# A Mamba-2 (SSD) scan stage: the sample sequences' states by products on quarters of the rows, and the D x term by VectorE

## The chip, the cores and the metric

One core of a Trainium2 chip runs the whole kernel in one launch. The metric is the device time of that core in microseconds (us), shown as the median of several runs.

## The reference, cut to what matters

One step of an encoder with two layers: a Mamba-2 mixer and a PEER channel mixer, then sliding-window attention and a second PEER mixer. Only the scan of the first layer is touched. `x` is the convolved input, `z` the gate; 32 heads of 64 columns stand in 8 groups of 4.

```python
def ssd_scan(x, dt, A, B, C, s0, block):
    acum = jnp.cumsum(dt * A.reshape(G, R), axis=2)
    lmat = jnp.exp(jnp.where(causal, seg, -jnp.inf))
    xdt = x * dt[..., None]
    cb = jnp.einsum('bcign,bcjgn->bcijg', C, B)
    y_diag = jnp.einsum('bcijgr,bcjgrp->bcigrp', cb[..., None] * lmat, xdt)
    decay_end = jnp.exp(acum[:, :, -1:] - acum)
    states = jnp.einsum('bcjgn,bcjgrp->bcgrpn', B, xdt * decay_end[..., None])
    # s = dec * s + st over the blocks; s_prev is the state before a block
    y_off = jnp.einsum('bcign,bcgrpn->bcigrp', C, s_prev) * jnp.exp(acum)[..., None]
    y = (y_diag + y_off)
# mamba_mixer:
    y = y + xs.astype(f32) * d_skip.astype(f32)[:, None]     # the D x term
    y = y.reshape(bsz, L, SSM_INNER) * jax.nn.silu(z.astype(f32))
    y = rmsnorm(y, norm_g)
    return y @ w_out, s_new, conv_new
```

There are 384 tokens: two blocks of 128 of one prompt, and one block that holds 8 sample sequences of 16 tokens. Each sample sequence has a state of its own, so the last block has 8 states per group, each 128 x 256.

## The kernel before, in words

The functions run one after another: `mamba()`, the first PEER mixer, `attention()`, the second PEER mixer. The order of the instructions on each engine isn't that of the code: a scheduler lays out the program by times that it estimates, and only instructions wrapped in `pin` keep the order of the code among each other. PSUM is one pool of 8 banks (`bank`).

Matmuls with weights are done in three fp32r products of high and low halves (L130 to L132); the halves are made by ScalarE (L105) and VectorE (L106). In `mamba()` a loop runs over the 8 groups. For each group:

- `b_tile`, `c_tile` and two `x_tile`s: each is a `conv_tile`, 24 matmuls (L130 to L132), then a convolution of four taps (VectorE L371) and a silu on ScalarE. POOL copies a few columns for the convolution's state (L362, L365, L366), and `c_tile` has it spread C for the sample sequences (L409).
- `gate`: 72 matmuls with w_z (L425 to L427), silu on ScalarE into `zs`.
- `fetch`: loads the row of the decay sums into `ab` (L391) and the sample states `s0` (L394, 1 MB), and has POOL write two diagonal matrices `dg` of D (L397).
- `decay`: 12 VectorE instructions on `ab` (L438), Exp on ScalarE (L441), C·B (L444), their product (L446), and B transposed (L449). `Bt` has 2 slices for the prompt's blocks and 8 for the sample block, each with the rows of one sequence and zeros elsewhere (8 ScalarE copies, L453).
- `tokens`: x transposed (L461), times dt and times the decay to the end, `xdt` and `xde` (VectorE L463).
- `states` (L471 to L475), and `outputs`: `pY` sums, for each half of each block, one product with the diagonal (L483, which is the D x term) and two products of `ab` and `xdt` (L487). `pO` takes the states' share: one product for prompt block 1 (L490), and for the sample block 8 products on 32 columns each (L494). VectorE then forms y in four steps: pO times the decay (L499), block 0 (L501), plus pY (L502), times the gate (L503). ScalarE squares y (L505).
- `turn`: y transposed, two banks of three blocks each (L512), split into `yhi`, `ylo` (ScalarE L108, VectorE L109).
- `carry`: s0 times its decay (VectorE L518), 8 products of full 128 rows with the masked `Bt` (L523), four additions (L525).
- `store`: the states go out by SP's queue (L528, L529, 1 MB).

The outputs, turn and carry of a group stand in the code between the tiles of the next group; those of the last group stand between the terms of the GEMM with w_out (`out_terms`), whose accumulators `accs` hold 6 of the 8 banks until the hidden state h is updated (L600). Then the first PEER mixer squares h (ScalarE L164), normalises it (VectorE L839, tile `qTp`), transposes it (L850) and starts its GEMM with p_w_q (L130 to L132 on `qhi`, `qlo`).

Of the kernel before, what the change touches and what calls it, by code (L numbers as in the profile page):

```python
# [9 lines left out]
F32 = mybir.dt.float32  # L10
# [5 lines left out]
AF = mybir.ActivationFunctionType  # L16
OP = mybir.AluOpType
AX = mybir.AxisListType

P = 128  # L20
D = 1024
KD = D // P
NB = 3
NP = 256
NT = NB * P
NSEQ = 8
# [32 lines left out]
def encoder_step(ctx: ExitStack, tc: tile.TileContext, t_in, t_out):  # L59
# [149 lines left out]
    def mamba(h_src):  # L209
        with ExitStack() as c:  # L210
# [42 lines left out]
            alog = brow(t_in["a_log"], HEADS, one, "alog")  # L253
            ng = T(one, [P, 16], F32, tag="ng")
            sync.dma_start(ng, t_in["m_norm"])
            dsk = T(one, [P, 16], F32, tag="dsk")
            sync.dma_start(dsk, t_in["d_skip"])

            ylo = T(y_pool, [P, 16, NT], F32R, tag="ylo")
            yhi = T(y_pool, [P, 16, NT], F32R, tag="yhi")  # L260
# [7 lines left out]
            decS = T(one, [P, NSEQ, HEADS], F32, tag="decS")  # L268
            rows = T(dram, [HEADS, NB, P], F32, tag="acum_rows")
            seqm = T(one, [P, NSEQ], F32, tag="seqm")  # L270
            msk = T(one, [P, NB, P], F32, tag="msk")
            CMS = []
            for i in range(2):
# [3 lines left out]
            if True:  # L277
                def steps():
# [11 lines left out]
                    same = T(one, [P, P], F32, tag="same")  # L290
                    dve.tensor_scalar(same, fif, seqf, None, op0=OP.is_equal)
                    dve.tensor_scalar(seqm, iob[:, :NSEQ], seqf, None, op0=OP.is_equal)
                    ones = T(one, [P, P], F32, tag="ones")
                    pool.memset(ones, 1.0)
                    tri = T(one, [P, P], F32, tag="tri")
# [84 lines left out]
                class Group:  # L380
# [6 lines left out]
                    def fetch(self):  # L387
                        g = self.g
                        self.ab = T(two, [P, 4, NB, P], F32, tag="ab")
                        src = rows[4 * g:4 * g + 4]  # L390
                        sync.dma_start(self.ab, bass.AP(tensor=src.tensor, offset=src.offset,  # L391
                                                        ap=[[0, P], [1, 4 * NB * P]]))
                        self.s0 = T(two, [P, NSEQ, 256], F32, tag="s0")
                        sync.dma_start(self.s0, t_in["state_ssm"][g])  # L394
                        self.dg = T(two, [P, 2, P], F32, tag="dg", bufs=1)
                        for j in range(2):
                            pool.tensor_scalar(self.dg[:, j], ident, dsk[:, 2 * g + j:2 * g + j + 1], None, op0=OP.mult)  # L397

                    def b_tile(self):
                        self.BT = T(two, [P, NT], F32, tag="BT")  # L400
# [31 lines left out]
                    def decay(self):  # L432

                        g, BT, CT = self.g, self.BT, self.CT
                        ab = self.ab
                        for rr in range(4):
                            for b in range(NB):
                                dve.scalar_tensor_tensor(ab[:, rr, b], ab[:, rr, b],  # L438
                                                         acum[:, b, 4 * g + rr:4 * g + rr + 1], msk[:, b],
                                                         op0=OP.subtract, op1=OP.add)  # L440
                        act.activation(ab, ab, AF.Exp)  # L441
                        cb = bank([P, NB, P])
                        for b in range(NB):
                            pe.matmul(cb[:, b], BT[:, b * P:(b + 1) * P], CT[:, b * P:(b + 1) * P],  # L444
                                      start=True, stop=True)
                        dve.tensor_tensor(ab, ab, cb[:, None].to_broadcast([P, 4, NB, P]), op=OP.mult)  # L446
                        pb = bank([P, NB, P])
                        for b in range(NB):
                            pe.transpose(pb[:, b], BT[:, b * P:(b + 1) * P], ident)  # L449
                        self.Bt = Bt = T(two, [P, 2 + NSEQ, P], F32, tag="Bt", bufs=1)  # L450
                        act.copy(Bt[:, 0:2], pb[:, 0:2])
                        for i in range(NSEQ):
                            act.activation(Bt[:, 2 + i], pb[:, 2], AF.Copy, scale=seqm[:, i:i + 1])  # L453

                    def tokens(self):
                        self.xdt = T(two, [P, NB, 256], F32, tag="xdt", bufs=1)
                        self.xde = T(two, [P, NB, 256], F32, tag="xde", bufs=1)
                        for b in range(NB):
                            px = bank([P, 256])
                            for j in range(2):  # L460
                                pe.transpose(px[:, j * P:(j + 1) * P], self.xs[:, j, b * P:(b + 1) * P], ident)  # L461
                            for o, sc in ((self.xdt, dt), (self.xde, ddt)):
                                dve.tensor_tensor(heads(o[:, b]), heads(px),  # L463
                                                  sc[:, b, self.hs].unsqueeze(2).to_broadcast([P, 4, 64]), op=OP.mult)

                    def states(self):

# [9 lines left out]
                    def outputs(self):  # L477
                        g = self.g
                        pY = [bank([P, 256]), bank([P, 2, 256])]
                        for b in range(NB):  # L480
                            o = pY[0] if b == 0 else pY[1][:, b - 1]
                            for j in range(2):
                                pe.matmul(o[:, j * P:(j + 1) * P], self.xs[:, j, b * P:(b + 1) * P], self.dg[:, j],  # L483
                                          start=True, stop=False)
                                for rr in (2 * j, 2 * j + 1):
                                    cs = slice(64 * rr, 64 * rr + 64)
                                    pe.matmul(o[:, cs], self.ab[:, rr, b], self.xdt[:, b, cs], start=False,  # L487
                                              stop=(rr == 2 * j + 1))
                        pO = bank([P, 2, 256])
                        pe.matmul(pO[:, 0], self.CT[:, P:2 * P], self.st[:, 0], start=True, stop=True)  # L490
                        for w in range(2):
                            for q in range(4):
# [1 line left out]
                                pe.matmul(pO[rows, 1], self.CM[:, w, q].rearrange("p w t -> p (w t)"),  # L494
                                          self.s0[:, 2 * q + w], start=(w == 0), stop=(w == 1),
                                          tile_position=(0, 32 * q))
                        y = self.y = T(two, [P, NB, 256], F32, tag="y", bufs=1)
                        y12 = y[:, 1:].rearrange("p b (r d) -> p b r d", d=64)
                        dve.tensor_tensor(y12, pO.rearrange("p b (r d) -> p b r d", d=64),  # L499
                                          etok[:, :, self.hs].unsqueeze(3).to_broadcast([P, 2, 4, 64]), op=OP.mult)  # L500
                        dve.tensor_tensor(y[:, 0], self.zs[:, 0], pY[0], op=OP.mult)  # L501
                        dve.tensor_tensor(y[:, 1:], y[:, 1:], pY[1], op=OP.add)  # L502
                        dve.tensor_tensor(y[:, 1:], y[:, 1:], self.zs[:, 1:], op=OP.mult)  # L503
                        for b in range(NB):
                            act.activation(self.zs[:, b], y[:, b], AF.Square, accum_out=ssq[:, b, g:g + 1])  # L505

# [8 lines left out]
                    def carry(self):  # L515
# [3 lines left out]
                                          s0.rearrange("p s (r d) -> p s r d", d=64),  # L519
                                          decS[:, :, self.hs].unsqueeze(3).to_broadcast([P, NSEQ, 4, 64]), op=OP.mult)  # L520
                        pss = [bank([P, 2, 256]) for _ in range(4)]
                        for i in range(NSEQ):
                            pe.matmul(pss[i // 2][:, i % 2], self.Bt[:, 2 + i], self.xde[:, 2], start=True, stop=True)  # L523
                        for k in range(4):
                            dve.tensor_tensor(s0[:, 2 * k:2 * k + 2], s0[:, 2 * k:2 * k + 2], pss[k], op=OP.add)  # L525

# [738 lines left out]
def _layout(i):  # L1265
# [20 lines left out]
    a["conv_b"] = f["m_conv_b"][0].reshape(32, P).T  # L1286
    a["dt_bias"] = f["m_dt_bias"][0]
    a["a_log"] = f["m_a_log"][0]
    a["d_skip"] = np.repeat(f["m_d_skip"][0], 64).reshape(16, P).T
    a["m_norm"] = f["m_norm"][0].reshape(16, P).T  # L1290
    a["w_out"] = f["m_w_out"][0]
    a["state_conv"] = f["state_conv"][0].reshape(NSEQ, 3, 32, P).transpose(3, 2, 0, 1)
# [54 lines left out]
```

## Time and profile before

| what | value |
|---|---|
| time, median of 3 runs (lowest to highest) | 2598.19 us (2575.7 to 2599.0) |
| the profiled execution: its time, its span | 2597.6 us, 2595.9 us |
| its mean granted TensorE clock | 0.976 of full speed |
| PE busy | 2449.1 us, 94% |
| DVE busy | 1941.7 us, 75% |
| ACT busy | 1323.8 us, 51% |
| POOL busy | 685.0 us, 26% |

PE is TensorE (a matmul of fp32 operands stands in the trace as two records), DVE VectorE, ACT ScalarE, POOL GpSimd, SP the queue engine that issues most transfers. The span is the time between the first and the last instruction of the profiled execution; its own time, 1.7 us longer, holds what lies around it. The scan of the 8 groups runs from about 30 to 330 us of the span, the GEMM with w_out to about 398 us.

### The profile page before, as it was taken

How to read it: one execution, taken by the hardware profiler on the slowest of the kernel's cores; microseconds unless marked ns; L12 is line 12 of the kernel's file. 1: busy time of each engine (PE TensorE's matmuls, PEld its weight loads, DVE VectorE, ACT ScalarE, POOL GpSimd, SP SyncE). 2: the span in 40 equal slices, each digit the busy share in tenths (PEclk: the TensorE clock that was granted, in tenths of full speed). 3: DMA queues.
4: the chain of work that ended last, by engine and by line, in shares of the span. 5: the costliest groups of instructions: out<-in, count | busy, mean ns of one | idle time of the engine just before them, and what ended most of it. 6: DMA issues, size and time to landing. Idle time of an engine off the chain costs nothing. (4 is left out here: it accounts for less than half of the span.)

```text
span 2595.9 us, 45141 instructions
## 1 busy us (share of the span) xinstructions
PE 2449.1 (94%) x16792; PEld 2070.4 (80%) x16792; DVE 1941.7 (75%) x4301; ACT 1323.8 (51%) x2562; POOL 685.0 (26%) x749
## 2 busy tenths in 40 slices
PE   7999999999899989999998999999899998899998
PEld 7999988988799966666666878998789976666666
DVE  6877737989899988765545655989989988775545
ACT  5655524433466665554444543434456666464444
POOL 2222200033322244333321100023332234433331
PEclk9999999999999999999998969999999999999999
DMA  4544444488888899888985204478888898988886
GB/s 182 203 148 178 144 135 145 151 282 273 271 305 293 292 340 349 330 308 296 322 307 179 92 9 150 137 253 280 269 286 287 296 323 311 364 294 294 321 315 233
DMA packets 179116, 645.62 MB, mean 249 GB/s; under 512 B 24192, under 2 KB 26096, under 8 KB 176240
## 3 DMA queue, kind: packets, MB, share of 16 engines
q1 hardware_dynamic: 99632, 366.90, 40.2%
q0 software_dynamic: 79264, 275.84, 30.5%
q8 instruction: 131, 2.15, 0.3%
q14 instruction: 89, 0.73, 0.1%
HBM read 626.43 MB, written 18.06 MB: 248 GB/s over the span
## 5 line engine op out<-in xcount | busy, mean ns | idle before, releaser
L105 ACT CAST hi<-raw 128x1024 fp32r<-128x1024 f32 (+1 forms) x616 | 641.3, 1042 | 652.8 <-PE bank L131 407.4
L106 DVE TENSOR_TENSOR lo<-raw,hi 128x1024 fp32r<-128x1024 f32 (+1 forms) x616 | 748.8, 1216 | 225.2 <-ACT hi L105 213.6
L1035 POOL DMA_INDIRECT gath<-in_p_u,eidU x256 | 301.9, 1179 | 803.3 <-DVE gath L1072 438.8
L132 PE MATMUL bank<-xhi,lo 128*128 128x256 f32 (+1 forms) x1344 | 407.5, 304 | 9.9 <-DVE lo L106 9.7
L130 PE MATMUL bank<-xhi,hi 128*128 128x256 f32 (+1 forms) x1344 | 402.3, 299 | 4.2 <-ACT hi L105 4.2
L131 PE MATMUL bank<-xlo,hi 128*128 128x256 f32 (+1 forms) x1344 | 396.7, 295 | 0.0
L132 PE MATMUL bank<-qhi,lo 128*128 128x256 f32 (+1 forms) x1152 | 348.9, 305 | 27.1 <-DVE lo L106 26.9
L130 PE MATMUL bank<-qhi,hi 128*128 128x256 f32 (+1 forms) x1152 | 348.1, 302 | 20.4 <-ACT hi L105 13.6
L1072 DVE SCALAR_TENSOR_TENSOR gath<-gath,xg 128x1024 f32<-128x1024 f32 x256 | 311.5, 1217 | 44.0 <-DMA gath<-in_p_u,eidU 43.9
L131 PE MATMUL bank<-qlo,hi 128*128 128x256 f32 (+1 forms) x1152 | 343.9, 299 | 0.0
L143 PE MATMUL bank<-lo,phi 128*128 128x512 f32 x1024 | 332.3, 406 | 10.2 <-DVE lo L106 8.2
L143 PE MATMUL bank<-hi,plo 128*128 128x512 f32 x1024 | 323.9, 398 | 0.0
L143 PE MATMUL bank<-hi,phi 128*128 128x512 f32 x1024 | 292.8, 406 | 19.4 <-ACT hi L105 16.1
L105 ACT CAST phi<-G 128x256 fp32r<-128x256 f32 x256 | 103.4, 405 | 382.0 <-PE bank L143 264.4
L1035 POOL DMA_INDIRECT gv<-in_p_v,eidT x180 | 202.1, 1123 | 319.0 <-PE bank L1089 273.6
L132 PEld LDWEIGHTS bank<-xhi,lo 128*128 128x128 f32 x1344 | 253.8, 189 | 18.0 <-DVE lo L106 14.1
L143 PEld LDWEIGHTS bank<-hi,phi 128*128 128x128 f32 x1024 | 186.9, 190 | 98.7 <-ACT hi L105 45.6
L130 PEld LDWEIGHTS bank<-xhi,hi 128*128 128x128 f32 x1344 | 254.3, 189 | 8.6 <-ACT hi L105 5.6
L131 PEld LDWEIGHTS bank<-xlo,hi 128*128 128x128 f32 x1344 | 254.1, 189 | 0.2
L132 PEld LDWEIGHTS bank<-qhi,lo 128*128 128x128 f32 x1152 | 222.9, 194 | 34.0 <-DVE lo L106 33.7
L143 PEld LDWEIGHTS bank<-lo,phi 128*128 128x128 f32 x1024 | 187.4, 190 | 73.2 <-DVE lo L106 18.3
L130 PEld LDWEIGHTS bank<-qhi,hi 128*128 128x128 f32 x1152 | 223.7, 194 | 24.3 <-ACT hi L105 16.7
(340 smaller groups left out, 3949.0 us busy)
## 6 DMA issues: line engine op xcount, KB each, us to landing
raw<-in_u_t SPq DMA_DIRECT2D x256, 512.0 KB
raw<-in_p_v SPq DMA_DIRECT2D x256, 512.0 KB
raw<-in_w_in SPq DMA_DIRECT2D x32, 512.0 KB
raw<-in_p_w_q SPq DMA_DIRECT2D x32, 512.0 KB
s<-in_state_ssm SPq DMA_DIRECT2D x8, 1024.0 KB
raw<-in_w_z SPq DMA_DIRECT2D x16, 512.0 KB
out_sm_ssm<-s SPq DMA_DIRECT2D x8, 1024.0 KB
raw<-in_w_out SPq DMA_DIRECT2D x16, 512.0 KB
```

Of the source, the lines that this page charges most:

```text
L105: act.copy(hi, raw)
L106: dve.tensor_tensor(lo, raw, hi32, op=OP.subtract)
L130: pe.matmul(ps, whi[:, s], xhi[:, k, c0:c1], start=(k == 0), stop=False)
L131: pe.matmul(ps, whi[:, s], xlo[:, k, c0:c1], start=False, stop=False)
L132: pe.matmul(ps, wlo[:, s], xhi[:, k, c0:c1], start=False, stop=(k == KD - 1))
L143: mm = pe.matmul(ps, x, w[:, hf * n:(hf + 1) * n], start=s_, stop=e_)
L1035: pool.indirect_dma_start(out=tile_, out_offset=None, in_=tab, in_offset=bass.IndirectOffsetOnAxis(ap=idx, axis=0))
L1072: pin(dve.scalar_tensor_tensor(tile_, tile_, 1.0, xg[g], op0=OP.mult, op1=OP.mult, accum_out=au[g][:, j:j + 1]))
```

## The change

The D x term leaves TensorE. `d_skip` is loaded as a row of 32 values, `dg` and its POOL instructions go, and so do the 48 products with it; `tokens` has VectorE write x times D into `y`, from the bank that it also reads for `xdt` and `xde`. `outputs` then adds: pO times the decay goes to a new tile `yo`, POOL adds `yo` to blocks 1 and 2 of `y`, VectorE adds the two pY banks and multiplies all three blocks by the gate in one instruction.

The states of the sample sequences: two sequences stand in each quarter of 32 rows. `Bt` now has two masked slices, one with the even and one with the odd sequences (mask `parm`). A product takes 32 rows of `Bt` and of `xde`, in the quarter q of the array's rows. The 8 products are pinned: all four quarters of the even sequences, each into its own bank, then the four of the odd ones.

```diff
-            dsk = T(one, [P, 16], F32, tag="dsk")
-            sync.dma_start(dsk, t_in["d_skip"])
+            dsk = brow(t_in["d_skip"], HEADS, one, "dsk")
...
+                    dve.tensor_reduce(parm, seqm.rearrange("p (q w) -> p w q", w=2), axis=AX.X, op=OP.add)
...
-                        self.dg = T(two, [P, 2, P], F32, tag="dg", bufs=1)
-                        for j in range(2):
-                            pool.tensor_scalar(self.dg[:, j], ident, dsk[:, 2 * g + j:2 * g + j + 1], None, op0=OP.mult)
...
-                        self.Bt = Bt = T(two, [P, 2 + NSEQ, P], F32, tag="Bt", bufs=1)
+                        self.Bt = Bt = T(two, [P, 4, P], F32, tag="Bt", bufs=1)
                         act.copy(Bt[:, 0:2], pb[:, 0:2])
-                        for i in range(NSEQ):
-                            act.activation(Bt[:, 2 + i], pb[:, 2], AF.Copy, scale=seqm[:, i:i + 1])
+                        for w in range(2):
+                            act.activation(Bt[:, 2 + w], pb[:, 2], AF.Copy, scale=parm[:, w:w + 1])
...
+                            dve.tensor_tensor(heads(self.y[:, b]), heads(px),
+                                              dsk[:, self.hs].unsqueeze(2).to_broadcast([P, 4, 64]), op=OP.mult)
...
-                            for j in range(2):
-                                pe.matmul(o[:, j * P:(j + 1) * P], self.xs[:, j, b * P:(b + 1) * P], self.dg[:, j],
-                                          start=True, stop=False)
-                                for rr in (2 * j, 2 * j + 1):
-                                    cs = slice(64 * rr, 64 * rr + 64)
-                                    pe.matmul(o[:, cs], self.ab[:, rr, b], self.xdt[:, b, cs], start=False,
-                                              stop=(rr == 2 * j + 1))
+                            for rr in range(4):
+                                cs = slice(64 * rr, 64 * rr + 64)
+                                pe.matmul(o[:, cs], self.ab[:, rr, b], self.xdt[:, b, cs], start=True, stop=True)
...
-                        y = self.y = T(two, [P, NB, 256], F32, tag="y", bufs=1)
-                        y12 = y[:, 1:].rearrange("p b (r d) -> p b r d", d=64)
-                        dve.tensor_tensor(y12, pO.rearrange("p b (r d) -> p b r d", d=64),
+                        y = self.y
+                        yo = T(two, [P, 2, 256], F32, tag="yo", bufs=1)
+                        dve.tensor_tensor(yo.rearrange("p b (r d) -> p b r d", d=64),
+                                          pO.rearrange("p b (r d) -> p b r d", d=64),
                                           etok[:, :, self.hs].unsqueeze(3).to_broadcast([P, 2, 4, 64]), op=OP.mult)
-                        dve.tensor_tensor(y[:, 0], self.zs[:, 0], pY[0], op=OP.mult)
+                        pool.tensor_tensor(y[:, 1:], y[:, 1:], yo, op=OP.add)
+                        dve.tensor_tensor(y[:, 0], y[:, 0], pY[0], op=OP.add)
                         dve.tensor_tensor(y[:, 1:], y[:, 1:], pY[1], op=OP.add)
-                        dve.tensor_tensor(y[:, 1:], y[:, 1:], self.zs[:, 1:], op=OP.mult)
+                        dve.tensor_tensor(y, y, self.zs, op=OP.mult)
...
-                        for i in range(NSEQ):
-                            pe.matmul(pss[i // 2][:, i % 2], self.Bt[:, 2 + i], self.xde[:, 2], start=True, stop=True)
+                        for w in range(2):
+                            for q in range(4):
+                                rows = slice(32 * q, 32 * q + 32)
+                                pin(pe.matmul(pss[q][:, w], self.Bt[rows, 2 + w], self.xde[rows, 2],
+                                              start=True, stop=True, tile_position=(32 * q, 0)))
```

Lines after the edits stand a few lines lower: L499, L502 and L503 of before answer to L497, L502 and L503, L438 to L437, L490 to L488, L494 to L492, L523 to L525, L525 to L528, L529 to L532, L600 to L603, L839 to L842, L850 to L853.

The scheduler lays the instructions out anew. On TensorE, in the turn of a group in mid-program (group 5), before: `xhi`, `xlo` rows are the conv tiles' matmuls (24 to a tile, shortened here), `ident` rows the transposes of `y`.

```order
L490 MATMUL bank_2787<-st_2760,CT_2397 128x256
L494 MATMUL bank_2787<-s_373_2347,cm_55_248 32x256 x8
L130 MATMUL bank_2806<-xhi_100,hi_2809 128x384
...
L132 MATMUL bank_2806<-xhi_100,lo_2810 128x384
L512 MATMUL bank_2853<-ident_69,y_2797 128x128
L512 MATMUL bank_2859<-ident_69,y_2797 128x128
...
L523 MATMUL bank_2912<-xde_2691,Bt_2587 128x256 x2
...
L512 MATMUL bank_2853<-ident_69,y_2797 128x128 x2
L512 MATMUL bank_2859<-ident_69,y_2797 128x128 x2
```

The same place now:

```order
L488 MATMUL bank_2725<-st_2704,CT_2346 128x256
L492 MATMUL bank_2725<-s_374_2304,cm_56_249 32x256 x8
L130 MATMUL bank_2745<-xhi_100,hi_2748 128x384
...
L132 MATMUL bank_2745<-xhi_100,lo_2749 128x384
L512 MATMUL bank_2792<-ident_69,y_2635 128x128 x3
L512 MATMUL bank_2798<-ident_69,y_2635 128x128 x3
L130 MATMUL bank_2805<-xhi_100,hi_2808 128x384
...
L525 MATMUL bank_2851<-xde_2634,Bt_2536 128x256
L525 MATMUL bank_2852<-xde_2634,Bt_2536 128x256
```

Before, one transpose per bank (block 0) stands behind the next conv tile's 24 matmuls, and the other four behind a second conv tile and the states' products. Now all six stand behind the first conv tile. Group 0 has all six directly behind the products of pO.

On VectorE at the same place, from pO's first reader on, before:

```order
L499 TENSOR_TENSOR y_2797<-bank_2787,etok_240 128x512
L518 TENSOR_TENSOR s_373_2347<-s_373_2347,decS_242 128x2048
L502 TENSOR_TENSOR y_2797<-y_2797,bank_2768 128x512
L438 SCALAR_TENSOR_TENSOR ab_3161<-ab_3161,acum_238,msk_245 128x128 x12
L503 TENSOR_TENSOR y_2797<-y_2797,zs_2684 128x512
```

and now (L502 waits for POOL's addition, L500, which waits for L497):

```order
L497 TENSOR_TENSOR yo_2735<-bank_2725,etok_240 128x512
L518 TENSOR_TENSOR s_374_2304<-s_374_2304,decS_242 128x2048
L502 TENSOR_TENSOR y_2635<-y_2635,bank_2712 128x512
L437 SCALAR_TENSOR_TENSOR ab_3098<-ab_3098,acum_238,msk_246 128x128 x12
L503 TENSOR_TENSOR y_2635<-y_2635,zs_2627 128x768
```

The order is the same; the last step now covers block 0 too, so that no block of y is ready before it. Groups 1 to 5 read so; in group 6 the 12 L437 don't stand ahead of L503.

On VectorE at the end of the w_out GEMM: before, h is updated (L600) and normalised (L839) without a break:

```order
L600 SCALAR_TENSOR_TENSOR h_90<-bank_3525,rs_3993,h_90 128x512
L600 SCALAR_TENSOR_TENSOR h_90<-bank_3526,rs_3993,h_90 128x512
L839 TENSOR_SCALAR qTp_4025<-h_90,rstd_4030 128x1024
...
L600 SCALAR_TENSOR_TENSOR h_90<-bank_3527,rs_3993,h_90 128x512
L600 SCALAR_TENSOR_TENSOR h_90<-bank_3528,rs_3993,h_90 128x512
L839 TENSOR_SCALAR qTp_4025<-h_90,rstd_4030 128x1024
```

and now:

```order
L603 SCALAR_TENSOR_TENSOR h_90<-bank_3454,rs_3915,h_90 128x512
L166 TENSOR_TENSOR ss_3950<-ss_627_3951 128x1
L528 TENSOR_TENSOR s_494_3100<-s_494_3100,bank_3677 128x512
L167 TENSOR_SCALAR ss_3950<-ss_3950 128x1
L528 TENSOR_TENSOR s_494_3100<-s_494_3100,bank_3678 128x512
L528 TENSOR_TENSOR s_494_3100<-s_494_3100,bank_3679 128x512
L528 TENSOR_TENSOR s_494_3100<-s_494_3100,bank_3680 128x512
L603 SCALAR_TENSOR_TENSOR h_90<-bank_3455,rs_3915,h_90 128x512
L166 TENSOR_TENSOR ss_3950<-ss_627_3951 128x1
L167 TENSOR_SCALAR ss_3950<-ss_3950 128x1
L842 TENSOR_SCALAR qTp_3947<-h_90,rstd_3952 128x1024 x3
```

The last group's states' products now fill four banks at once, and two of the four come free only when h is updated; the last six of the eight products stand behind nearly all of the w_out GEMM, the additions between the updates of h, and all three L842 behind them. The first L842 waits, besides, for the store of these states (L532), because its tile lies where the scan's buffers lay. Before, that store stood some 30 us earlier.

## Rows read from the trace of the kernel before

**Rows 1.** The page: each engine's busy time, share of the span and instructions.
```profile
PE 2449.1 (94%) x16792; PEld 2070.4 (80%) x16792; DVE 1941.7 (75%) x4301; ACT 1323.8 (51%) x2562; POOL 685.0 (26%) x749
```

**Rows 2.** Busy time of the engines in stretches of the scan: from:to, length in us, then busy us of PE, weight loads, DVE, ACT, POOL with instruction counts, PE's granted clock, DMA share, GB/s.
```profile
80.00:130.00 50.00, 49.48 (x354) 47.22 (x353) 42.15 (x74) 34.60 (x75) 8.98 (x26) 1.00 0.59 214
...
230.00:280.00 50.00, 50.00 (x360) 48.48 (x360) 40.37 (x65) 32.48 (x73) 12.89 (x31) 1.00 0.52 188
```

**Rows 3.** The timeline of PE in one group: start us, us, engine, line, operation, tiles, shape, count of records.
```profile
213.72 0.44 PE L483 MATMUL bank<-dg,xs 128*128 128x128 f32 x2
214.00 0.56 PE L487 MATMUL bank<-xdt,ab 128*128 128x64 f32 x4
214.39 0.44 PE L483 MATMUL bank<-dg,xs 128*128 128x128 f32 x2
...
216.31 1.07 PE L494 MATMUL bank<-s,cm 128*32 128x256 f32 x16
217.31 0.45 PE L130 MATMUL bank<-xhi,hi 128*128 128x384 f32 x1
...
221.58 0.38 PE L512 MATMUL bank<-ident,y 128*128 128x128 f32 x2
...
226.04 3.62 PE L523 MATMUL bank<-xde,Bt 128*128 128x256 f32 x16
229.49 0.60 PE L512 MATMUL bank<-ident,y 128*128 128x128 f32 x4
```

**Rows 4.** Groups of instructions of the first 620 us, shapes kept apart: line, engine, operation, tiles, shapes, count | busy us, mean ns of one | idle before.
```profile
L523 PEld LDWEIGHTS bank<-xde,Bt 128*128 128x128 f32 x128 | 24.1, 190 | 3.1
L397 POOL TENSOR_SCALAR dg<-ident,dsk 128x128 f32<-128x128 f32 x16 | 11.4, 720 | 11.7 <-PE bank L483 11.7
L463 DVE TENSOR_TENSOR xde<-bank,ddt 128x256 f32<-128x256 f32 x24 | 9.9, 414 | 0.0
```

**Rows 5.** The timeline of DVE in the same group (columns as in rows 3; in brackets the idle time before, and who ended it).
```profile
217.45 0.69 DVE L499 TENSOR_TENSOR y<-bank,etok 128x512 f32<-128x512 f32 x1 [1.43 <-PE bank L494]
218.06 2.28 DVE L518 TENSOR_TENSOR s<-s,decS 128x2048 f32<-128x2048 f32 x1
220.25 0.68 DVE L502 TENSOR_TENSOR y<-y,bank 128x512 f32<-128x512 f32 x1
220.85 3.23 DVE L438 SCALAR_TENSOR_TENSOR ab<-ab,acum,msk 128x128 f32<-128x128 f32 x12
224.01 0.68 DVE L503 TENSOR_TENSOR y<-y,zs 128x512 f32<-128x512 f32 x1
224.61 1.21 DVE L106 TENSOR_TENSOR lo<-raw,hi 128x1024 fp32r<-128x1024 f32 x1
```

**Rows 6.** The timeline of POOL there.
```profile
216.47 0.60 POOL L397 TENSOR_SCALAR dg<-ident,dsk 128x128 f32<-128x128 f32 x1
...
222.99 2.88 POOL L365 COPY cst<-xp 128x3 f32<-128x3 f32 x1 [5.72 <-ACT xp L363]
...
228.78 0.19 POOL L365 COPY cst<-xp 128x3 f32<-128x3 f32 x1 [2.34 <-ACT xp L363]
...
232.95 0.41 POOL L409 COPY cm<-CT 128x64 f32<-128x64 f32 x2 [1.95 <-ACT CT L374]
```

**Rows 7.** The timeline of PE in group 0's turn.
```profile
73.30 1.07 PE L494 MATMUL bank<-s,cm 128*32 128x256 f32 x16
...
74.58 3.62 PE L523 MATMUL bank<-xde,Bt 128*128 128x256 f32 x16
77.85 0.53 PE L130 MATMUL bank<-xhi,hi 128*128 128x384 f32 x1
```

**Rows 8.** The timeline of DVE there.
```profile
82.38 1.28 DVE L525 TENSOR_TENSOR s<-s,bank 128x512 f32<-128x512 f32 x2
83.58 0.68 DVE L503 TENSOR_TENSOR y<-y,zs 128x512 f32<-128x512 f32 x1
```

**Rows 9.** PE after a gap, at the start of the first PEER mixer.
```profile
406.64 0.69 PE L130 MATMUL bank<-qhi,hi 128*128 128x384 f32 x1 [3.63 <-ACT xf L852]
...
410.33 0.52 PE L132 MATMUL bank<-qhi,lo 128*128 128x384 f32 x1
410.65 0.47 PE L130 MATMUL bank<-qhi,hi 128*128 128x384 f32 x1
```

**Rows 10.** Stretches around two gaps of PE of 3.6 and 3.2 us (columns as in rows 2).
```profile
403.00:411.00 8.00, 4.37 (x15) 4.36 (x15) 6.47 (x10) 6.14 (x15) 0.00 (x0) 0.57 0.49 170
...
2119.00:2123.00 4.00, 0.84 (x8) 0.17 (x10) 2.72 (x4) 0.53 (x1) 0.93 (x1) 1.00 1.03 416
```

**Rows 11.** The timeline of DVE at the end of the w_out GEMM.
```profile
392.32 1.41 DVE L600 SCALAR_TENSOR_TENSOR h<-bank,rs,h 128x512 f32<-128x512 f32 x2 [1.13 <-PE bank L143]
...
401.11 0.75 DVE L839 TENSOR_SCALAR qTp<-h,rstd 128x1024 f32<-128x1024 f32 x1 [0.65 <-POOL rstd L168]
```

**Rows 12.** SP's queue: a store of a group's states, and the next load into the same buffer, which waits for it; twice.
```profile
120.22 0.34 SPq L529 DMA_DIRECT2D out_sm_ssm<-s  x1
124.43 0.33 SPq L394 DMA_DIRECT2D s<-in_state_ssm  x1
...
194.87 0.34 SPq L529 DMA_DIRECT2D out_sm_ssm<-s  x1
200.39 0.33 SPq L394 DMA_DIRECT2D s<-in_state_ssm  x1
```

More of the change, by code (lines that the diff above doesn't have):

```diff
@@ L270, in mamba @@
             seqm = T(one, [P, NSEQ], F32, tag="seqm")
+            parm = T(one, [P, 2], F32, tag="parm")
             msk = T(one, [P, NB, P], F32, tag="msk")
@@ L457, in tokens @@
                         self.xde = T(two, [P, NB, 256], F32, tag="xde", bufs=1)
+                        self.y = T(two, [P, NB, 256], F32, tag="y", bufs=1)
                         for b in range(NB):
@@ L1288, in _layout @@
     a["a_log"] = f["m_a_log"][0]
-    a["d_skip"] = np.repeat(f["m_d_skip"][0], 64).reshape(16, P).T
+    a["d_skip"] = f["m_d_skip"][0]
     a["m_norm"] = f["m_norm"][0].reshape(16, P).T
```

## The prediction

> **What bounds the kernel now.** I read the page first: PE is busy 94% of the span, DVE 75% [rows 1]. That average hides stages, so the stretches of the scan came next. There PE is busy 49.5 to 50.0 of every 50 us at a granted clock of 1.00, with DVE at 40 to 42, ACT at 32 to 35 and POOL at 9 to 13 [rows 2]. In the scan PE sets the time: work taken off PE shortens it, work put on DVE costs nothing until PE has to wait for it. So the question is what PE waits for after the change, and the order of the instructions answers more of it than the list of operations.
>
> **TensorE's work removed.** A product with the diagonal and the two with `ab` behind it repeat every 0.67 us (213.72, 214.39), and the diagonal's part is 0.28 (213.72 to 214.00) [rows 3]. Its two records go. A group has six such patterns of six records at 0.112 each; twelve records less are 1.34 us, of which I take 1.28, since the first pattern has products of L471 in it and was never so dense. The states' products take 3.45 us (226.04 to 229.49), 0.216 a record. Their 16 records remain, but four quarters of rows may run beside each other. No row has that. The nearest has 16 records on four quarters of columns, L494: 1.00 us from its start to the next start (216.31 to 217.31), after which the first matmul is drawn out to 0.45 [rows 3]. With 0.16 for that change of form, an estimate from the 0.45, the block would take 1.16, a saving of 2.29. From the other side, quarters that don't overlap cost what they cost now, 3.45, and the change of form: a saving of -0.2. I take 1.16, because L494 is the row nearest in kind and size. Per group PE loses 1.28 + 2.29 = 3.57 us of work; over 8 groups 28.6.
>
> What the quarters don't share with L494 is the weights, 32 x 128 instead of 128 x 32; a load of 128 columns takes 190 ns [rows 4]. The Trainium skill, "TensorE: Matmul & The Clock Gate", Part 3, measured 3.07 times the speed for four row quarters at 512 columns; by that alone the block would be 3.45 / 3.07 = 1.12 us, an estimate beside my 1.16. Its Part 2 says that the time of a weight load goes with its columns, not its rows, so that 16 loads could be the longer part; no row here has a quarter's load.
>
> **TensorE's new wait.** The transposes of y stand right behind the first conv tile now, as the order shows, and they need all of y. PE reaches them 4.20 us after pO is done (217.38 to 221.58) [rows 3]. When is y done? DVE starts on pO at 217.45, goes on to L518 at 218.06, L502 at 220.25, the twelve L438 at 220.85 and L503 at 224.01 [rows 5]. In steps: 0.07, 0.61, 2.19, 0.60, 3.16. L503 now covers 768 columns; 512 take 0.60 from start to start, 256 take 0.33 by the L463 rows less overlap (0.41 [rows 4]), so 0.95 with its end. Without POOL that is 7.6 us.
>
> Between L518 and L502 comes POOL's addition. No row shows it. Below, 64 columns copied in 0.24 against 3 columns in 0.19 [rows 6] make 0.8 ns a column, 0.6 us for 512; above, L397's 0.60 for 128 columns [rows 6] (0.72 as a mean, with its hold-ups [rows 4]) times four is 2.4. I take 1.0, nearer the copies, since the added columns stream like theirs and L397's time holds a fixed start. Does it hide beside L518? A POOL copy of 3 columns started at 222.99 and took 2.88 us, until 225.87; DVE ran the L438 row, L503 and L106 all that time, each with two operands in SBUF, and L106 ended at 225.82. The same copy took 0.19 elsewhere [rows 5, 6]. So POOL stands still while such a row of DVE instructions runs, and L518 is one of them. The addition then starts only when L518 ends, while L502 waits for it: 1.0 + 0.1 for the hand-offs. The Trainium skill, "SBUF — State Buffer", section "Who interferes with whom", states this as an exclusive lock between a VectorE instruction with two SBUF inputs and a GpSimd one that reads SBUF; by that rule the addition is exposed whole, without it not at all, and the 2.88 agrees with it.
>
> So y is done 8.7 us after pO, and PE stands 8.76 - 4.20 = 4.6 us. What is queued behind the transposes on PE is ready conv work that can't pass. Before, that wait did not exist: the four late transposes stood at 229.49, after L503's end at 224.69 [rows 3, 5].
>
> The idle time has a price of its own. After 3.63 us without work PE came back with matmuls 0.32 us apart instead of 0.178 (24 in 4.27 us, rows 3), the granted clock being 0.57 over that stretch, 1.2 GHz for most of it, until 410.65 [rows 9, 10]. Thirteen matmuls at 0.32 cost 13 x 0.15 = 2.0 us more. Another gap of 3.2 us, at 2119, left the clock at 1.00 [rows 10], so this is likely at 4.6 us, not sure. Groups 1 to 5: 4.6 + 2.0 - 3.57 = +3.0 each, +15.2 in all.
>
> **Group 0** has its transposes directly behind pO. DVE is busy without a break there, and its queue before L503 changes little: two L525 (1.20) go behind, one L438 (0.27) and 0.27 of L503 come in. Before, L503 ended at 84.26, so y is done at 83.6 [rows 8]. Before, PE had the states' products behind it at 77.85 [rows 7]. Now they follow the transposes: 83.6 + 0.06 + 0.5 + 1.16 = 85.3, 7.45 later, less 0.36 for the transposes that no longer come afterwards: +7.1, and +2.0 for the clock, +9.1.
>
> **Group 6** has no L438 row ahead of L503: y is done 3.16 sooner, PE stands 1.35, below the gaps that lowered the clock: 1.35 - 3.57 = -2.2. **Group 7** lies inside the w_out GEMM, which gives PE work ahead of the transposes: the diagonal's 1.28 are saved; of 2.29 some 1.4 go again since the products are torn into three pieces with changes of form between: -2.2.
>
> **The end of the w_out GEMM.** The last states' products come so late that their four additions (0.68 each as L502, a same-shaped one) stand between the updates of h, and the store is issued after them. Before, the first update starts at 392.32, and the last normalisation L839 ends at 401.86, 9.5 later [rows 11]. Now: six updates (4.1), the additions (2.7) and waits for PE's last pieces (1.9) and for the small steps, about 9.4 to the store's issue. The same 1 MB store kept the next load waiting 4.2 (120.22 to 124.43) and 5.5 us (194.87 to 200.39) [rows 12]. Only then does the first of three L842 start; they take 2.0. That is 9.4 + 4.2 to 5.5 + 2.0 = 15.6 to 16.9, 6 to 7.4 later than before; +6.5, with 4 and 9 as ends. Everything after this point hangs on it: no other work is ready.
>
> **Costs at nothing.** Three more DVE instructions per group in `tokens` (24 in all, 0.33 each from start to start) lie beside the conv tile and stand ahead of nothing that PE has reached; without that cover they would cost 1.0 a group. The 48 ScalarE copies and 16 POOL writes less stand on engines that are busy 70% and 26% at most. The row of D and the mask come once, before the scan.
>
> **The sum.** 15.2 + 9.1 - 2.2 - 2.2 + 6.5 = +26.4 on the profiled execution's 2597.6: 2624.0. Its time is 0.6 under the median of 2598.19, so the two are the same here. A measurement of this kernel can tell about 1% from no change, 2572 to 2624: my forecast lies on the upper bound.
>
> **The rivals.** (1) Forecast as above, 0.46; its own range 2612 (the clock does not fall in five groups, -10 or -12) to 2634.
>
> (2) Not slower: POOL's addition runs beside L518. For it: POOL's spans are rough, and it may start first, as L497 hands over before L518 begins. Against it: the 2.88. Place: groups 1 to 6, price 1.1 a group; PE then stands 3.5 us, as long as what it saves, and at that length the clock fell after 3.63 and not after 3.2. From the point where the stall stays under that, groups 1 to 5 give -0.1 each, group 0 +7.1, group 6 -3.3, group 7 -2.2 and the end +6.5: 2605, nothing that can be measured. 0.28.
>
> (3) The quarters don't gain, because weight loads or the array's rows don't overlap: 2.29 x 7 groups = +16 on the forecast, 2640. For it: the weights are four times as wide as L494's. Against: nothing but the likeness. 0.12.
>
> (4) POOL's addition costs as L397 does, 2.4: +1.4 in each of five groups, 2631. For it: the only arithmetic of POOL in the scan. 0.10.
>
> (5) Faster: PE never waits, all 28.6 come in and only the end costs: 2597.6 - 28.6 + 6.5 = 2576. It needs y 4.2 us after pO; L518 and the L438 row alone take 5.35. 0.04.
>
> **How the numbers follow.** Half of (1), all of (3) and (4) are over 2624: 0.23 + 0.22 = 0.45 slower; half of (1) and (2) are within: 0.51; (5) is faster. The range takes in (2) and (3) and leaves out (5) and worse mixtures: 2600 to 2643.
>
> **What would show it.** Right: gaps of PE before L512 of 4 to 5 us in groups 1 to 5 that VectorE's y ends, about 10 in group 0; granted clock under 1.00 in the scan; POOL's L500 running to well after L518's end; 16 records of L525 within 1.2 us; the first L842 idle on a DMA. Wrong: L525 at 3 us or more (rival 3), L500 done by L518's end (rival 2), or L512 without a gap (rival 5).

## The result and the profile after

| | before | after |
|---|---|---|
| median (lowest to highest) | 2594.28 us (2575.70 to 2599.00, 4 runs) | 2626.91 us (2619.66 to 2630.52, 4 runs) |
| ratio, 95% interval | | 1.0127 [1.0092, 1.0162] |
| span of the profiled execution | 2595.9 us | 2618.0 us |
| first product with p_w_q starts at | 406.64 us [rows 9] | 434.69 us |
| from there to the end of the span | 2189.3 us | 2183.3 us |

Slower by 1.3%, 2.9 us over the predicted 2624.0. I use the start of the first product with p_w_q as the mark below: all that the change touches lies ahead of it. Behind it the profiled executions of all versions here spread from 2179 to 2202 us, with no relation to the edits. So the mark tells terms of a few us apart; a time does not. Each mark comes from one traced execution. How well such a start repeats is seen once: a version below has the same program as the changed kernel up to the last group, and the last group's products on columns (L492) start at 358.44 us there and at 357.64 here.

The page after, PE's line, and the stretches of the scan that answer to [rows 2] (same columns).

```profile
PE 2434.1 (93%) x16696; PEld 2049.3 (78%) x16696; DVE 1952.8 (75%) x4326; ACT 1312.4 (50%) x2514; POOL 690.3 (26%) x741
```
```profile
80.00:130.00 50.00, 40.46 (x276) 37.32 (x277) 33.48 (x61) 26.96 (x55) 8.19 (x20) 0.86 0.42 150
...
230.00:280.00 50.00, 45.44 (x320) 42.26 (x318) 38.29 (x63) 24.23 (x52) 14.14 (x24) 0.93 0.49 164
```

PE has less to do over the span (2434 against 2449), and yet in the scan it stands 4.6 to 9.5 us in each 50 at a clock below 1.00, where before it stood 0.5 us at most, at 1.00.

Starts that are used below: the products on columns of groups 1 and 7 before, then those of the changed kernel and its mark.

```profile
103.69 1.07 PE L494 MATMUL bank<-s,cm 128*32 128x256 f32 x16
...
334.30 1.07 PE L494 MATMUL bank<-s,cm 128*32 128x256 f32 x16
```
```profile
110.39 1.07 PE L492 MATMUL bank<-s,cm 128*32 128x256 f32 x16
...
357.64 1.07 PE L492 MATMUL bank<-s,cm 128*32 128x256 f32 x16
...
434.69 0.44 PE L130 MATMUL bank<-qhi,hi 128*128 128x384 f32 x1 [2.89 <-ACT xf L855]
```

The timelines of PE, DVE and POOL in one group (group 4), for [rows 3], [rows 5] and [rows 6]:

```profile
233.61 1.07 PE L492 MATMUL bank<-s,cm 128*32 128x256 f32 x16
243.67 1.51 PE L512 MATMUL bank<-ident,y 128*128 128x128 f32 x6 [4.56 <-DVE y L503]
...
250.64 1.15 PE L525 MATMUL bank<-xde,Bt 32*128 32x256 f32 x16
```
```profile
234.75 0.69 DVE L497 TENSOR_TENSOR yo<-bank,etok 128x512 f32<-128x512 f32 x1
235.35 2.28 DVE L518 TENSOR_TENSOR s<-s,decS 128x2048 f32<-128x2048 f32 x1
238.82 0.69 DVE L502 TENSOR_TENSOR y<-y,bank 128x512 f32<-128x512 f32 x1 [1.18 <-POOL y L500]
239.42 3.23 DVE L437 SCALAR_TENSOR_TENSOR ab<-ab,acum,msk 128x128 f32<-128x128 f32 x12
242.57 0.95 DVE L503 TENSOR_TENSOR y<-y,zs 128x768 f32<-128x768 f32 x1
```
```profile
235.52 3.27 POOL L500 TENSOR_TENSOR y<-y,yo 128x512 f32<-128x512 f32 x1 [0.47 <-DVE yo L497]
```

The transposes wait 4.56 us for the last step of y; of DVE's chain, 1.18 is the wait for POOL. The 16 records of the quarters span 1.15, against 3.62. Group 0, for [rows 7], and the end of the w_out GEMM, for [rows 11]:

```profile
71.74 1.07 PE L492 MATMUL bank<-s,cm 128*32 128x256 f32 x16
83.24 1.51 PE L512 MATMUL bank<-ident,y 128*128 128x128 f32 x6 [10.43 <-DVE y L503]
```
```profile
411.99 1.41 DVE L603 SCALAR_TENSOR_TENSOR h<-bank,rs,h 128x512 f32<-128x512 f32 x2 [1.12 <-PE bank L143]
...
425.59 2.08 DVE L842 TENSOR_SCALAR qTp<-h,rstd 128x1024 f32<-128x1024 f32 x3 [2.16 <-DMA out_sm_ssm<-s]
```

### The profile page after: what moved, and what is told of

The parts are those of the page before. It is cut to its first block, busy times and chain, and to the rows that moved or that the text cites. A ratio compares the mean times of both kernels' runs of the same rounds, so it can differ in the third digit from the quotient of the medians.

```text
span 2618.0 us, 44922 instructions
## 1 busy us (share of the span) xinstructions
PE 2434.1 (93%) x16696; PEld 2049.3 (78%) x16696; DVE 1952.8 (75%) x4326; ACT 1312.4 (50%) x2514; POOL 690.3 (26%) x741
## 5 line engine op out<-in xcount | busy, mean ns | idle before, releaser
L106 DVE TENSOR_TENSOR lo<-raw,hi 128x1024 fp32r<-128x1024 f32 (+1 forms) x616 | 749.6, 1218 | 256.6 <-ACT hi L105 255.7
L106 DVE TENSOR_TENSOR plo<-G,phi 128x256 fp32r<-128x256 f32 x256 | 108.5, 424 | 178.3 <-PE bank L143 163.1
```

The source lines that it names most:

```text
L106: dve.tensor_tensor(lo, raw, hi32, op=OP.subtract)
```

## The experiments

The theory: PE saves what was reckoned, and loses more by standing at three places: ahead of the transposes in groups 1 to 6, there in group 0, and at the end, behind a late store. The rivals: the quarters cost something, POOL is slow, or VectorE is the bound. The runs D x alone, L518 behind y and last group bank by bank were timed twice each, the others 8 or 12 times.

| run | median us | ratio to before, 95% | first p_w_q product |
|---|---|---|---|
| D x alone | 2637.37 | 1.0154 [1.0124, 1.0183] | 446.85 |
| quarters alone | 2592.54 | 0.9987 [0.9963, 1.0010] | 407.00 |
| L518 behind y | 2620.61 | 1.0089 [1.0060, 1.0118] | 427.47 |
| transposes late | 2599.89 | 1.0024 [1.0009, 1.0039] | 405.64 |
| L518 and L437 behind y | 2604.91 | 1.0040 [1.0016, 1.0063] | 421.67 |
| last group bank by bank | 2623.45 | 1.0108 [1.0062, 1.0154] | 430.02 |
| all three | 2599.22 | 1.0017 [1.0000, 1.0034] | 414.59 |
| order repaired | 2586.15 | 0.9962 [0.9943, 0.9982] | 389.98 |
| quarters repaired | 2595.92 | 0.9995 [0.9974, 1.0015] | 395.07 |

**D x alone.** The states' products and the masked copies of before put back:

```diff
-                        for w in range(2):
-                            for q in range(4):
...
+                        for i in range(NSEQ):
+                            pe.matmul(pss[i // 2][:, i % 2], self.Bt[:, 2 + i], self.xde[:, 2], start=True, stop=True)
```

> The D x term by VectorE alone; the states' products stay 8 products on all 128 rows, with the 8 masked slices of B, in the old order (bank by bank). Measured by the start of the first product with p_w_q (before 406.64 us, changed kernel 434.69), since what comes later varies by some us from build to build. My theory (the wait of PE for the late transposes of y comes from the D x part, the quarters only save): the gap before the transposes stays at 4 to 5 us in groups 1 to 5 with the clock falling after it, each group costs 2.3 us more than in the changed kernel (+16), and the end of the w_out GEMM is as before the change, since the bank-by-bank order lets the last group's store go early (-6.5): about 444, the time near 2636. Rival (the pinned quarters are what hurts): no gaps in groups 1 to 5, a start at 395 to 405, the time near 2590.

```profile
255.24 1.51 PE L512 MATMUL bank<-ident,y 128*128 128x128 f32 x6 [4.57 <-DVE y L503]
...
446.85 0.69 PE L130 MATMUL bank<-qhi,hi 128*128 128x384 f32 x1 [3.62 <-ACT xf L852]
```

The gaps are there without the quarters, and the whole loss with them: the mark is 40.2 later than before the change. It came 2.9 later than expected.

**Quarters alone.** The reverse: the diagonal, `dg` and y as before, products and `Bt` as changed.

> The states' products on quarters alone; the products with the diagonal stay. My theory: in groups 1 to 6 only block 0 is transposed early, no gap there, 2.3 us less per group (-14 in all, period 35.25 us instead of 37.54); group 0 has all six transposes directly behind pO and keeps a gap of about 10 us (+9); the last group's states' products are late and the first normalisation of h waits for the store (+6.5): the first product with p_w_q at about 409, the time within 0.5% of the kernel before. Rival (the quarters cost what they save or more in steady groups, by weight loads or changes of form): period 37.5 or more, start at 423 or later.

```profile
83.83 1.12 PE L514 MATMUL bank<-ident,y 128*128 128x128 f32 x4 [7.55 <-DVE y L505]
...
227.42 1.15 PE L527 MATMUL bank<-xde,Bt 32*128 32x256 f32 x16
228.50 0.66 PE L514 MATMUL bank<-ident,y 128*128 128x128 f32 x4
...
398.94 1.30 PE L855 MATMUL bank<-ident,qTp 128*128 128x128 f32 x5 [6.69 <-DVE qTp L844]
```

The period (from the products on columns of one group to those of the next) is 35.42 us (217.68 to 253.10), 2.12 less than 37.54, and no gap over 0.31 stands in groups 1 to 6. A gap in group 0 (7.55 us) and the wait at the end stay. The products take 1.08 to the next start instead of 3.45; 0.10 ahead of them and 0.06 behind, at the changes of form, come off the saving. The quarters do what they should. Their price is the new order in the first and the last group, where the stretches are 6.1 and 5.7 us longer than before (36.50 against 30.39, 78.01 against 72.34).

**L518 behind y.** One rule of order, `yend` being the last step of y:

```diff
+                        with tc.issue_after(self.yend.ins):
                             dve.tensor_tensor(s0.rearrange("p s (r d) -> p s r d", d=64),
```

> The changed kernel with one more rule of order: on VectorE the decay of the sample states (L518) comes behind the last step of y, so that POOL's addition has no L518 beside it. Two theories of the 3.27 us that the addition takes: (lock) it stands still while L518 runs with two operands in SBUF, and takes 1.2 us by itself; (slow) it takes 3.3 us anyway. Lock: L500 at 1.1 to 1.3 us, y done 3.5 us after pO, no gap before the transposes in groups 1 to 5, the first product with p_w_q at about 392, the time near 2585. Slow: L500 at 3.2 to 3.3, y done 5.5 us after pO, gaps of 1.3 us without a lower clock, the first product at about 402, the time near 2595.

One line of the trace by source, first of the changed kernel, then of this run: count, shortest, median and longest duration in ns. Then DVE's timeline.

```profile
L500 POOL TENSOR_TENSOR y<-y,yo x8: 3235/3266/3269, 73.6 to 359.6; 128x512 f32<-128x512 f32 x8
```
```profile
L500 POOL TENSOR_TENSOR y<-y,yo x8: 1261/1297/1299, 73.0 to 352.8; 128x512 f32<-128x512 f32 x8
```
```profile
234.90 0.69 DVE L502 TENSOR_TENSOR y<-y,bank 128x512 f32<-128x512 f32 x1 [1.41 <-POOL y L500]
236.69 2.72 DVE L437 SCALAR_TENSOR_TENSOR ab<-ab,acum,msk 128x128 f32<-128x128 f32 x10 [1.09 <-DMA ab<-acum_rows]
239.32 0.95 DVE L503 TENSOR_TENSOR y<-y,zs 128x768 f32<-128x768 f32 x1
```

The addition takes 1.30 us with L518 gone from its side and 3.27 beside it, where it ended 1.16 us after L518 (238.79 against 237.63). So it stood still while L518 ran. The slow theory is out. But VectorE waits for POOL either way: 1.18 us beside L518, 1.41 with nothing beside the addition. The gaps did not go as expected: the scheduler put ten L437 ahead of L503 again, 3.3 to 4.8 us stayed in groups 1 to 5, and the mark came at 427.47, where one theory had 392 and the other 402.

**Transposes late.** `carry` called before `turn`, the transposes pinned:

```diff
-                        prev.turn()
...
                         prev.carry()
+                        prev.turn()
```

> The changed kernel with the transposes of y moved behind the states' products of the same group (carry before turn in the code, the transposes pinned among the pinned products); VectorE and POOL do what they did. My theory (only the place of the transposes on PE makes the loss): no gap in groups 1 to 5, no lower clock there, a group's period 37.54 - 3.57 = 34.0 us; group 0 keeps most of its gap, the wait for the store of the last group stays: the first product with p_w_q at about 399 us, the time near 2590. Rival (VectorE is the bound, the wait only moves elsewhere): the period stays over 36 us, the gaps stand before other instructions, the start at 415 or later.

```profile
193.65 1.15 PE L525 MATMUL bank<-xde,Bt 32*128 32x256 f32 x16
194.73 0.87 PE L512 MATMUL bank<-ident,y 128*128 128x128 f32 x6
...
206.25 0.39 PE L425 MATMUL bank<-lo,xhi 128*128 128x256 f32 x1 [0.43 <-DVE lo L106]
```

With VectorE and POOL doing the same, the gaps of groups 1 to 6 and the low clock there are gone, and the mark is 29 us earlier, though group 0's gap is still 11.7: in groups 1 to 6 the place of the transposes on PE was the loss. Yet the period is 34.8 (218.89 to 253.72), not 34.0, and the mark 6.6 later than expected. The block of products of states and `ab` is 1.34 shorter than in the run with the quarters alone. But the gate's products take 0.5 longer, since PE stands 0.43 there for VectorE's L106, and the rest is hundredths at many places. So the D x part is worth 35.4 - 34.8 = 0.6 a group here.

**L518 and L437 behind y.** The same rule on the twelve L437 as well.

> The changed kernel with two rules of order on VectorE: the decay of the sample states (L518) and the next group's twelve L437 both come behind the last step of y. PE's order keeps the transposes behind the first conv tile. My theory (the gap is the length of VectorE's and POOL's chain from pO to the last step of y): y is done 0.07 + 0.61 + 1.41 + 0.60 + 0.95 = 3.6 us after pO, under the 4.2 at which PE comes; no gap and no lower clock in groups 1 to 6, a period of 34.8 us as with the transposes moved on PE, group 0's gap about 4 to 6 instead of 10.4, the store of the last group still late: the first product with p_w_q at 394 to 397 us, the time near 2585. Rival (VectorE has no room, what comes later is missed later): gaps of some us before the products of ab or other conv tiles, a period over 37.

PE's timeline, and two stretches behind two such gaps (columns as in [rows 2]):

```profile
203.58 0.71 PE L446 MATMUL bank<-CT,BT 128*128 128x128 f32 x4 [2.84 <-ACT CT L375]
...
278.16 1.22 PE L446 MATMUL bank<-CT,BT 128*128 128x128 f32 x4 [2.86 <-ACT CT L375]
```
```profile
203.58:208.00 4.42, 4.42 (x37) 4.42 (x38) 4.07 (x6) 2.60 (x9) 2.80 (x7) 1.00 0.94 332
278.16:282.60 4.44, 4.44 (x21) 4.44 (x22) 1.92 (x3) 3.43 (x10) 2.22 (x7) 0.50 0.72 276
```

The rival was right. No gap over 0.8 stands ahead of the transposes of groups 1 to 6, but one of 2.8 to 3.1 ahead of C times B in each: L518 and L437, together 5.3 us of VectorE's time, now stand behind y and ahead of the next tile's convolution. The run gives the price of the clock besides. Gaps of one length left it at 1.00 or at 0.50 in the rows above. The periods are 37.3 (222.16 to 259.46) with the first and 38.8 or 40.0 (146.05 to 184.88, 259.46 to 299.48) with the second, so a lower clock cost 1.5 to 2.7 us a time. The eight runs of this kernel spread over 24 us, and the traced one is the slowest, so this mark may be some us late.

**Last group bank by bank.** In the last group alone, `order.sort()` on the (q, w) pairs and no pin.

> The changed kernel with one edit: in the last group alone the eight products of the states go bank by bank (both products of a quarter after each other, not pinned), as they did before the change. Groups 0 to 6 as changed. My theory (the pinned order over four banks makes the store of the last group late, and the first normalisation of h waits for it): the store is issued some 30 us earlier, the first L842 doesn't wait for it, and the first product with p_w_q comes at 428 us instead of 434.7, with every group's gap as before; the time near 2620. Rival (the end of the w_out GEMM is late for another reason, such as the additions between the updates): 432 or later.

The store of the states on SP's queue in the changed kernel, then here; then DVE's first normalisation of h here, which is L846 in this version.

```profile
421.60 0.34 SPq L532 DMA_DIRECT2D out_sm_ssm<-s  x1
```
```profile
388.88 0.34 SPq L536 DMA_DIRECT2D out_sm_ssm<-s  x1
```
```profile
419.77 0.75 DVE L846 TENSOR_SCALAR qTp<-h,rstd 128x1024 f32<-128x1024 f32 x1
```

The store is issued 33 us earlier, and the first normalisation no longer waits for it: from the last group's L492 to the mark it is 71.6 us instead of 77.05 (72.34 before the change). The gaps of the groups are as before this edit (36.7 us in sum against 36.6), but the last group's L492 starts 0.8 later, so that the mark is 4.7 earlier where I expected 6.7. The time could not show it: behind the mark this execution took 2202 us.

**All three edits together.**

> A version to beat both: the changed kernel with the transposes of y behind the states' products (those of group 0 behind the next conv tile and C times B), L518 and the twelve L437 behind the last step of y, and the last group's states' products bank by bank. My theory adds up the three terms: no gap in any group (-6.5 x 5, -1.5), none in group 0 (-12), the end of the w_out GEMM as before the change (-6.5): the first product with p_w_q at about 385 us against 406.6 before the change, the time near 2576, a ratio of 0.992. Rival (the saving is given back later, where VectorE or the loads set the time): the same start near 385 but a time over 2590.

Missed: gaps of 2.9 to 3.7 us ahead of C times B came with the rule for L437, one of 4.2 stayed in group 0, and the mark stood at 414.59.

**Order repaired.** Late transposes (group 0's behind the gate) and the last group's order, no rule on VectorE.

> The changed kernel with the transposes of y behind the states' products (group 0's behind the gate's products), and the last group's states' products bank by bank; VectorE's order is left to the scheduler, with the twelve L437 ahead of the last step of y. After the last round the theory is that VectorE has no slack at this place: what is put behind y (L518, L437) makes the convolution of the next tile late, so only PE's order is to be changed. Expected: no gap over 1 us in the scan, a period of 34.8 us in groups 1 to 6, the end of the w_out GEMM as before the change, the first product with p_w_q at 386 to 390 us against 406.6 before the change, the time near 2580, a ratio of 0.994. Rival (later stages give the gain back, as they set their own pace by their loads): the same start, but a ratio of 1.00.

```profile
118.24 0.71 PE L443 MATMUL bank<-CT,BT 128*128 128x128 f32 x4 [2.30 <-ACT CT L375]
...
389.98 0.69 PE L130 MATMUL bank<-qhi,hi 128*128 128x384 f32 x1 [3.62 <-ACT xf L860]
```
```profile
118.24:122.60 4.36, 4.36 (x24) 4.36 (x25) 4.33 (x6) 3.54 (x10) 1.75 (x6) 0.61 0.60 195
```

This version beats both: 0.9962 [0.9943, 0.9982] of before, the mark 16.7 us earlier. No gap over 1 us was expected; from the first products on columns on, two remain: 1.29 in group 0 and 2.30 ahead of C times B in the next, with the clock at 0.61 behind it. From group 2 on the period is 34.8 to 35.1. The mark is where I expected it. Of its 16.7 us the time shows 10.5.

**Quarters repaired.**

> The quarters alone, without the D x part (the products with the diagonal stay), with group 0's transposes behind the gate's products and the last group's states' products bank by bank. Expected: a period of 35.4 us as in the run with the quarters alone, no gap in group 0 (-9.5) and no wait for the store (-6.3): the first product with p_w_q at about 391 us, the time near 2582, a ratio of 0.995; the D x part would then be worth 0.6 us a group, not the 1.3 that PE saves by it. Rival (the later stages give it back): a ratio of 1.00.

The period is 35.3, the mark 395.07, 11.6 before that of the kernel before, but 4 later than expected: against the run with the quarters alone the first stretch gained 6.7 instead of 9.5, with a gap of 2.02 left in group 0, and the last one 4.5 instead of 6.3. The time is not to be told from that of the kernel before. Here a mark 11.6 earlier moved the median by only 0.7 us, so the 10.5 of the version above can't be put down to the edits by the times alone. Between the last two versions lie some 0.45 us a group, which is what the D x part is worth in groups 2 to 6.

## Why the prediction was right

By the starts of the products on columns (L494, now L492), each stretch from one group's to the next's, and from the last to the mark:

| stretch | predicted | measured |
|---|---|---|
| up to group 1 (+9.1 less group 1's 1.28) | +7.8 | +6.7 (110.39 against 103.69) |
| groups 1 to 5 | 5 x 3.0 = +15.2 | +4.3, +3.4, +3.0, +3.4, +3.4 = +17.4 |
| group 6 | -2.2 | -0.7 |
| last group to the mark (+6.5 less 0.9) | +5.6 | +4.7 |
| sum at the mark | +26.4 | +28.05 |

The mechanism was as forecast at each of the three places. For groups 1 to 6 and for the end a run that moved that place alone shows it; for group 0 the two repaired versions do, where its gap of 10.43 us is gone (the largest left there behind the first products on columns are 1.29 and 2.02). Term by term:

- PE's saving: the ab block 1.34 (1.28 reckoned), the quarters 2.12 (2.29). Right; L494 was the row to go by.
- The stall in groups 1 to 5: 4.6 reckoned; 4.56 or 4.57 in three groups, 4.93 in group 2, where VectorE also waited 0.28 for the loading of `ab`, and 5.99 in group 1, where its convolution kept it from pO for 1.5 us. Right, but for these two.
- POOL's addition: exposed 1.1 reckoned, 1.18 measured; by itself 1.30, not 1.0. That it waits for L518 is shown by the run with L518 behind y, 3.27 us against 1.30. Here the rule of the Trainium skill ("SBUF — State Buffer", "Who interferes with whom") and the trace agree. L518 gives the addition no cover, and without L518 there is none either (1.41): what is exposed is about the addition's own length in both orders.
- The clock: 2.0 reckoned. In the group above, the six transposes and the nine matmuls up to 247.86 take 4.19 us, the matmuls 0.32 apart; in the run with L518 and L437 behind y the same take 2.23 at full speed, so it cost 1.96. In that run the price was 1.5 to 2.7. Group 0's clock fell too (0.55 from 83 to 88 us). One reading of the prediction does not hold: rival (2) and group 6 took the 3.63 and 3.2 us of [rows 10] as if a shorter gap left the clock alone, but in the version with the order repaired a gap of 2.30 was followed by 0.61.
- Group 6: the stall of 1.54 (1.35 reckoned; the prediction's own terms give 8.76 - 3.16 - 4.20 = 1.40) left the clock at 1.00. Of the 1.5 us missing, 0.85 is w_out work that now stands ahead of group 7's L492 instead of behind it. With these 0.85 the end comes to 5.6, the predicted size.
- The end: L842 waited for the store, and the row of L603 and L842 took 15.7 us (411.99 to 427.67), 15.6 to 16.9 reckoned. A further 2.2 us that I had not reckoned lies between L842 and the first product with p_w_q (7.02 against 4.78): all 24 transposes come at once, at a clock of 0.50 (426 to 432 us). That the end still came to 5.6 is luck: from L492 to the first update of h it is 3.67 us shorter than before (54.35 against 58.02), 0.85 of it the moved work, so 2.8 where 0.9 was reckoned, and the two errors cancel.
- Costs at nothing: right for the changed kernel, where PE has no other gap over 0.31 in groups 1 to 6. In the repaired one some 0.8 of the 1.34 that PE saves is lost again, in the main where PE waits for VectorE's L106. That VectorE's additional 1.3 us a group make L106 late is likely, but no run shows it.

Stretches behind the gaps of groups 4, 6 and 0 (columns as in [rows 2]):

```profile
243.60:248.60 5.00, 4.93 (x19) 4.96 (x20) 3.94 (x6) 4.61 (x12) 0.55 (x4) 0.57 0.31 108
322.00:327.00 5.00, 4.49 (x28) 4.53 (x29) 4.26 (x7) 3.18 (x11) 1.35 (x2) 1.00 0.34 107
83.00:88.00 5.00, 4.76 (x27) 3.67 (x28) 0.65 (x2) 4.97 (x11) 0.25 (x2) 0.55 0.00 0
```

Not settled: why the time behind the mark spreads by 23 us. The medians differ by 32.6 us, the marks by 28.05; the rest is within that spread. So it is in part luck that 2624.0 lies only 2.9 us from the median: the forecast added +26.4 to 2597.6, and the median of the kernel before is 2594.28 in the table above.

## What to carry to other kernels

Work taken off a full engine counts only as far as its new order adds no wait: look where the first reader of the changed tile stands, and how long the chain that writes it is in its own engines' queues. Here a saving of some 28 us of TensorE's work was lost to transposes that stood 4.6 us or more too early in groups 1 to 5 and 10 in group 0, to the lower clock behind them, and to a late store at the end. It came back in part (the mark 16.7 us earlier than before, the median 10.5) when the order was set by hand at two kinds of places. A GpSimd instruction put between two VectorE instructions cost VectorE a wait of 1.2 to 1.4 us, about its own length of 1.30: the two-operand VectorE instruction that ran beside it, 2.28 us long, hid none of it.

## What was not expected of the hardware

Gaps of PE of one length (2.84 and 2.86 us) were followed by a clock of 1.00 in one group and of 0.50 in another, so that a group's cost varies by 1.5 to 2.7 us at the same wait. A gap of 2.30 was followed by 0.61 in one version, and one of 3.2 us by 1.00 in the kernel before [rows 10], so the length of a gap alone does not tell. And four row quarters ran nearly as fast as four column quarters, 1.08 against 1.00 us for 16 records, though each loads weights of 128 columns (a median of 185 ns a load, beside 110 ns for the 32 columns of the other).
